# Stores of layer norms and of gated activations on other queues, and one sum of squares on the tensor engine

## The chip, the cores and the metric

The kernel runs on one core of a Trainium2 chip. A core has a tensor engine (PE, with its weight loads shown apart as PEld), a vector engine (DVE), a scalar engine (ACT), GpSimd (POOL) and a sync engine (SP) that only begins transfers. Each engine works through one queue of instructions in order. A transfer (DMA) is begun by an instruction on the queue of SP, ACT or POOL, and is then carried by 16 DMA engines that all queues share. The metric is the device time of one execution in microseconds (us). Three runs of the kernel before gave 3619.58, 3623.87 and 3626.42 us, median 3623.87 us.

## The reference, cut to what matters

Two layers are applied to two sequences, of 1040 and 272 positions (16 meta tokens ahead of each), with 1024 channels, all in float32. Layer 0 mixes tokens by a long convolution, layer 1 by attention. In each layer the mixer's result is added to the input and normed, and then a gated MLP with a convolution over three positions is added and normed again:

```python
h = layer_norm(DEEPNORM_ALPHA * h + m, ln1_g[i], ln1_b[i])
f = conv_ffn(h, ffn_w_in[i], ffn_conv_w[i], ffn_conv_b[i], ffn_w_out[i])
h = layer_norm(DEEPNORM_ALPHA * h + f, ln2_g[i], ln2_b[i])

def conv_ffn(x, w_in, conv_w, conv_b, w_out):
    h = x @ w_in
    g, a = jnp.split(h, 2, axis=-1)
    g = dwconv3(g, conv_w, conv_b)
    return (jax.nn.gelu(g, approximate=False) * a) @ w_out

def layer_norm(x, g, b):
    mu = mean(x); xc = x - mu; var = mean(xc * xc)   # over the 1024 channels
    return xc * rsqrt(var + LN_EPS) * g + b
```

## The kernel before, in words

Channels lie on the 128 partitions, in 8 tiles (index k or f), and positions in the free dimension. The positions are cut into four chunks: p = 0 has two of 384 columns, p = 1 two of 272 (layer 0) or 258 (layer 1); c = 0, 1 says which of the two. Every matrix product is taken in three passes over a high and a low part of each factor (lines 288 to 290), so weights and activations are first split: a copy on ACT (line 259) makes the high part, a subtraction on DVE (line 260) the low one.

A layer's second half has three stages.

`out_proj` (line 847 loads, 851 adds) makes the input of the first norm. `window_norms` norms the chunks of one p, stores the normed tiles to DRAM (`xd`, line 868) and makes the 7 operands T of the block product. It runs as work in the background: its pieces are traced between the matrix products of the next stage.

`ffn_in` multiplies T by weights (loaded at line 920), with convolution and gelu, and gates: `store` multiplies on DVE (line 985) and stores the gated tile to DRAM (`hd`, line 987), four stores for each of the 22 blocks of a layer. The first four blocks are done for p = 0 alone and then for p = 1 alone, while the norm of p = 1 still runs.

`ffn_out` reads back `hd` (line 1026, tile `hraw`, three buffers) and loads weights (line 1022), splits both, and accumulates for c = 0 and then for c = 1. The second norm of a c runs in the background of what follows; its results go to `x2d` in layer 0 (line 1403, after a split into the next input) and to the output `y` in layer 1 (line 1411).

`layer_norm` itself: the mean by a product with a constant matrix (line 781), subtraction on DVE (786), squares on ACT (788), their sum over the 8 tiles on POOL, one after another (790), the mean of that on PE (796), the reciprocal root in small steps on ACT and DVE (820 to 825), a broadcast on PE (804), and for each tile a scaling on DVE (809), a bias on ACT (810) and `done(f)`, which begins the store. `pin` puts a PE instruction behind everything that was traced on PE before it. The last two norms, of c = 1 in layer 1, have nothing beside them: the kernel ends with them.

The order on each queue is made by a planner, which issues the instructions by priority as they come ready in its own model; tiles, buffers and semaphores are its work as well. In the kernel before all of these stores are begun by SP, on the same queue as every load of weights and of `hraw`; the only transfers that POOL begins are in the first stage (lines 467 and 542), and ACT begins none.

Of the kernel before, what the change touches and what calls it, by code (L numbers as in the profile page):

```python
# [17 lines left out]
KC = D // 128  # L18
# [229 lines left out]
class Trunk:  # L248
# [519 lines left out]
        if f:  # L768
            self.nc.vector.tensor_tensor(out=sm, in0=A[0] if f == 1 else sm, in1=A[f], op=ALU.add)

    def layer_norm(self, A, sm, idx, done):


        nc = self.nc
        v = nc.vector
        n = sm.shape[-1]
        b = self.lnp[:, idx + 1]
        ps = lambda: self.pps.tile([128, 512], F32, tag="ln", name=self.n("ln"), bufs=2)[:, :n]
        mu = ps()
        pin = self.tc.keep_in_program_order  # L780
        pin(nc.tensor.matmul(out=mu, lhsT=self.o1024, rhs=sm, start=True, stop=True))
        nb = -(-n // 128)
        m = 2 * -(-n // (2 * nb))
        at = [min(m * i, n - m) for i in range(nb)]
        for f in range(KC):
            v.tensor_tensor(out=A[f], in0=A[f], in1=mu, op=ALU.subtract)
            sq = sm if f == 0 else self.tp(n)
            nc.scalar.activation(out=sq, in_=A[f], func=AF.Square)  # L788
            if f:
                nc.gpsimd.tensor_tensor(out=sm, in0=sm, in1=sq, op=ALU.add)  # L790
            if f == 3:
                yield 1.5
        yield 8
        var = ps()
        for i, o in enumerate(at):
            x = nc.tensor.matmul(out=var[:m, i:i + 1], lhsT=sm[:, o:o + m], rhs=self.o1024[:, 0:1], start=True, stop=True)
            if i == 0:
                pin(x)
        small = lambda: self.tmp.tile([128, 4], F32, tag="rs", name=self.n("rs"), bufs=6)[:m, :nb]
        r = self.rsqrt(small, var[:m, :nb], nb, self.eps[:m, 0:1], LN_EPS)  # L800
        yield 1.5
        rb = ps()
        for i, o in enumerate(at):
            x = nc.tensor.matmul(out=rb[:, o:o + m], lhsT=r[:, i:i + 1].to_broadcast([m, 128]), rhs=self.ident[:m, :m],
                                 start=True, stop=True)
            if i == 0:
                pin(x)
        for f in range(KC):
            v.scalar_tensor_tensor(out=A[f], in0=A[f], scalar=self.lng2[:, idx, f:f + 1], in1=rb, op0=ALU.mult, op1=ALU.mult)
            nc.scalar.activation(out=A[f], in_=A[f], func=AF.Identity, bias=b[:, f:f + 1])  # L810
            done(f)
            if f == 3:
                yield 3
# [42 lines left out]
    def window_norms(self, l, lay, p, A, sms, idx):  # L856

        nc = self.nc
        v = nc.vector
        n, n2 = lay.n[p], lay.n[p] + 2  # L860

        def done(c):
            o = lay.start[p][c]

            def f(k):
                for z in lay.zeros(p, lay.window(p, c)[0], n2):
                    nc.gpsimd.memset(A[c][k][:, z:z + 1], 0.0)
                nc.sync.dma_start(out=self.xd[l][:, k, o:o + n], in_=A[c][k][:, 1:n + 1])
            return f

        gens = [self.layer_norm(A[c], sms[c], idx, done(c)) for c in range(2)]
        while gens:
            for g in list(gens):
                x = next(g, None)
                if x is None:
                    gens.remove(g)
                else:
                    yield x / 2
        T = self.T[p] = {x: [] for x in PRODUCTS}
        left = 16  # L880

        def operand():
            nonlocal left
            left -= 1
            if left >= 0:
                return self.act.tile([128, 2, n2], F32R, tag=f"y{p}", name=self.n("T"), bufs=16)
            return self.tx.tile([128, 2, n2], F32R, tag=f"t{p}x", name=self.n("T"), bufs=(12, 16)[p])

        for q in range(2):
            for x in PRODUCTS:  # L890
                T[x].append((operand(), operand()))
            for j in range(2):
                k = 2 * q + j
                b11, b21, b12, b22 = A[0][k], A[0][k + 4], A[1][k], A[1][k + 4]
                put = lambda x, src: self.split(src, T[x][q][0][:, j], T[x][q][1][:, j])
                put("B11", b11)
                t2, t1 = self.tp(n2), self.tp(n2)
                v.tensor_tensor(out=b12, in0=b22, in1=b12, op=ALU.subtract)
                v.tensor_tensor(out=t2, in0=b12, in1=b11, op=ALU.add)
                put("B21", b21)  # L900
                put("T2", t2)
                v.tensor_tensor(out=t1, in0=b22, in1=t2, op=ALU.subtract)
                put("T1", t1)
                yield 2
                put("T3", b12)
                put("B22", b22)
                v.tensor_tensor(out=t2, in0=b21, in1=t2, op=ALU.subtract)
                put("T4", t2)
                yield 2
# [31 lines left out]
    def ffn_in(self, l):  # L941


        nc = self.nc
# [16 lines left out]
        for m, pairs in jobs:  # L961
            cw = self.cwf[:, l, m]
            st = {p: {} for p in pairs}
            for p in pairs:
                self.need(p)
            for x in PRODUCTS:
                while len(ready) < 4:
                    r = next(ops, None)
                    if r is None:
                        break  # L970
                    ready.append(r)
                wt = ready.pop(0)
                for p in pairs:
                    n, S = lay.n[p], st[p]
                    n2, T = n + 2, self.T[p][x]
                    mine = slice(1, n + 1)
                    key = dict(B11="a", T2="a", T3="a", T4="a", B21="b", T1="c", B22="c")[x]
                    new = x in ("B11", "B21", "T1")
                    if new:
                        S[key] = bank()[:, :n2]  # L980
                    ps = S[key]
                    self.mm3(ps, [(wt[k][0], wt[k][1], T[k // 2][0][:, k % 2], T[k // 2][1][:, k % 2]) for k in range(4)], new, again=not new)

                    def store(g, val, c):
                        v.tensor_tensor(out=g, in0=g, in1=val, op=ALU.mult)
                        o = 384 if p else 0
                        nc.sync.dma_start(out=self.hd[l][c, m, :, o:o + n], in_=g)

                    if x in ("B11", "T2", "T1"):
                        S[x] = self.tp(n2)  # L990
                        nc.scalar.copy(out=S[x], in_=ps)
                    elif x == "B21":
                        v.tensor_tensor(out=S["B11"], in0=S["B11"], in1=ps, op=ALU.add)
                        g = S["g"] = hidden(n)
                        self.conv3(g, S["B11"], n, cw)
                        nc.scalar.activation(out=g, in_=g, func=AF.Gelu)
                    elif x == "T3":
                        v.tensor_tensor(out=S["T1"][:, mine], in0=S["T1"][:, mine], in1=ps[:, mine], op=ALU.add)
                    elif x == "B22":
                        v.tensor_tensor(out=S["T2"], in0=S["T2"], in1=ps, op=ALU.add)  # L1000
                        g = hidden(n)
                        self.conv3(g, S["T2"], n, cw)
                        nc.scalar.activation(out=g, in_=g, func=AF.Gelu)
                        store(g, S["T1"][:, mine], 1)
                    else:
                        store(S["g"], ps[:, mine], 0)
                    self.tick(0.0055 * n2)

    def ffn_out(self, l, idx, done):
# [31 lines left out]
        for c in range(2):  # L1041
# [25 lines left out]
                        self.tick(0.9 * (k1 - k0))  # L1067
            for p in range(2):
                A = [z[:, 384 * p:384 * p + lay.n[p]] for z in C]
                self.later(("x", 2 * p + c), self.layer_norm(A, sms[p], idx, done(p, c, A)))  # L1070


    def qkv(self, common, later):
# [323 lines left out]
    def to_x(self, p, c, A):  # L1397
        lay = LAYERS[0]
        o, n, at = lay.start[p][c], lay.n[p], c * lay.n[p]

        def f(k):
            self.split(A[k], self.x[p][0][k][:, at:at + n], self.x[p][1][k][:, at:at + n])
            self.nc.sync.dma_start(out=self.x2d[:, k, o:o + n], in_=A[k])
        return f

    def to_y(self, p, c, A):
        s = p and c
        o = LAYERS[1].start[p][c] - LAYERS[1].col(s, T0)

        def f(k):  # L1410
            self.nc.sync.dma_start(out=self.a[f"y_{s}"][:, k, o:o + LAYERS[1].n[p]], in_=A[k])
        return f


# [18 lines left out]
```

## Time and profile before

| | us |
|---|---|
| median of three runs | 3623.87 |
| the profiled execution's own time | 3623.7 |
| its span (first to last instruction) | 3621.5 |
| PE busy | 3425.1 |
| DVE busy | 2290.0 |
| ACT busy | 1707.8 |
| POOL busy | 509.0 |

The times below are counted from the start of the span. Busy time is the time in which an engine executes; an instruction that begins a transfer takes time on its queue and is not counted as busy, except on POOL. "Idle before" an instruction is how long its engine had nothing to do, with what ended that. SPq, ACTq and POOLq are the queues of these engines.

### The profile page before, as it was taken

The numbers are of one execution on the slowest core, as the hardware profiler recorded it, in microseconds if no ns is written. First come the engines' busy times: TensorE is split into PE (matmuls) and PEld (weight loads), VectorE is DVE, ScalarE is ACT, GpSimd is POOL, SyncE is SP. The second block draws the span as 40 slices with busy tenths as digits, with TensorE's granted clock in tenths as the row PEclk, the third lists the DMA queues.
The fourth block names the chain that finished last, engine by engine and source line by source line (L and its number), as shares of the span: only waits on it lengthen the run. The fifth ranks groups of instructions, "written<-read, shape, count | busy, mean of one in ns | idle before, by whom it ended". The sixth has DMA issues, their size and how long they took to land.

```text
span 3621.5 us, 61578 instructions
## 1 busy us (share of the span) xinstructions
PE 3425.1 (95%) x23000; PEld 3315.7 (92%) x23000; DVE 2290.0 (63%) x4624; ACT 1707.8 (47%) x3614; POOL 509.0 (14%) x626
## 2 busy tenths in 40 slices
PE   8999999999989999999899999999979999999986
PEld 7999999998879999999898988888979999999986
DVE  6555554664797666654667557776598666654645
ACT  4333333663465444433545447776375444433434
POOL 2434341110110000000102341110110000000101
PEclk8999999999989999999999999999989999999998
DMA  6222223544222212255565440001233222246575
GB/s 169 89 96 91 92 89 114 146 136 139 94 87 92 74 61 75 67 178 178 158 195 166 135 130 16 16 12 44 92 102 97 77 68 66 74 135 203 139 196 139
DMA packets 239741, 391.69 MB, mean 108 GB/s; under 512 B 30580, under 2 KB 134235, under 8 KB 239059
## 3 DMA queue, kind: packets, MB, share of 16 engines
q1 hardware_dynamic: 232659, 364.70, 33.4%
q0 software_dynamic: 6784, 23.07, 1.7%
q8 instruction: 180, 2.95, 0.3%
q14 instruction: 118, 0.97, 0.1%
HBM read 302.22 MB, written 78.84 MB: 105 GB/s over the span
## 4 chain that ended last, share of the span: by engine, by line
PE 63%; DVE 5%; ACT 4%; DMA 2%; POOL 1%; issue 1%; SPq 0%; POOLq 0%; ACTq 0%; DVEq 0%
PE mm L288 17%; PE mm L290 17%; PE mm L289 17%; PE pt L1263 2%; PE sc L288 1%; PE pv L1279 1%; PE pv L1280 1%; DVE w L260 1%; PE pv L1281 1%; PE sc L290 1%; PE sc L289 1%; POOL tp L790 1%; DVE T L260 1%; DMA hraw<-hd 1%; ACT C L810 1%
## 5 line engine op out<-in xcount | busy, mean ns | idle before, releaser
L288 PE MATMUL mm<-T,w 128*128 128x386 f32 (+2 forms) x2464 | 778.0, 316 | 34.4 <-ACT w L259 26.7
L260 DVE TENSOR_TENSOR w<-raw,w 128x512 fp32r<-128x512 f32 (+2 forms) x744 | 511.9, 691 | 437.8 <-ACT w L259 424.3
L259 ACT CAST w<-raw 128x512 fp32r<-128x512 f32 (+2 forms) x744 | 439.1, 593 | 729.2 <-PE mm L289 571.8
L290 PE MATMUL mm<-T,w 128*128 128x386 f32 (+2 forms) x2464 | 774.7, 315 | 3.7 <-DVE w L260 3.4
L289 PE MATMUL mm<-T,w 128*128 128x386 f32 (+2 forms) x2464 | 774.6, 314 | 0.0
L288 PE MATMUL mm<-y,w 128*128 128x386 f32 (+6 forms) x1664 | 543.9, 327 | 14.3 <-ACT y L259 10.2
L290 PE MATMUL mm<-y,w 128*128 128x386 f32 (+6 forms) x1664 | 531.1, 320 | 12.9 <-DVE w L260 12.8
L289 PE MATMUL mm<-y,w 128*128 128x386 f32 (+6 forms) x1664 | 532.5, 320 | 2.6 <-DVE y L260 1.2
L288 PEld LDWEIGHTS mm<-T,w 128*128 128x128 f32 x2464 | 468.3, 190 | 41.9 <-ACT w L259 31.1
L290 PEld LDWEIGHTS mm<-T,w 128*128 128x128 f32 x2464 | 467.7, 190 | 7.8 <-DVE w L260 7.5
L289 PEld LDWEIGHTS mm<-T,w 128*128 128x128 f32 x2464 | 468.9, 190 | 0.3
L288 PE MATMUL mm<-hq,w 128*128 128x328 f32 (+2 forms) x1408 | 440.7, 317 | 23.6 <-ACT hq L259 23.4
L289 PE MATMUL mm<-hq,w 128*128 128x328 f32 (+2 forms) x1408 | 444.3, 316 | 7.0 <-DVE hq L260 7.0
L290 PE MATMUL mm<-hq,w 128*128 128x328 f32 (+2 forms) x1408 | 443.5, 315 | 0.0
L790 POOL TENSOR_TENSOR tp<-tp,tp 128x384 f32<-128x384 f32 (+5 forms) x112 | 116.7, 1050 | 1836.3 <-ACT tp L788 1830.2
L288 PEld LDWEIGHTS mm<-y,w 128*128 128x128 f32 x1664 | 321.3, 193 | 19.0 <-ACT y L259 12.9
L290 PEld LDWEIGHTS mm<-y,w 128*128 128x128 f32 x1664 | 321.5, 193 | 14.8 <-DVE w L260 14.3
L289 PEld LDWEIGHTS mm<-y,w 128*128 128x128 f32 x1664 | 321.3, 193 | 8.2 <-DVE y L260 3.9
L288 PEld LDWEIGHTS mm<-hq,w 128*128 128x128 f32 x1408 | 268.6, 192 | 25.0 <-ACT hq L259 24.9
L289 PEld LDWEIGHTS mm<-hq,w 128*128 128x128 f32 x1408 | 270.5, 192 | 8.8 <-DVE hq L260 8.5
L290 PEld LDWEIGHTS mm<-hq,w 128*128 128x128 f32 x1408 | 270.0, 192 | 0.0
L260 DVE TENSOR_TENSOR hq<-hraw,hq 128x656 fp32r<-128x656 f32 (+1 forms) x220 | 187.1, 851 | 62.4 <-ACT hq L259 58.2
(210 smaller groups left out, 5759.5 us busy)
## 6 DMA issues: line engine op xcount, KB each, us to landing
raw<-in_w_fin SPq DMA_DIRECT2D x208, 256.0 KB
hraw<-hd SPq DMA_DIRECT2D x110, 328.0 KB
hraw<-hd SPq DMA_DIRECT2D x110, 321.0 KB
raw<-in_w_fout SPq DMA_DIRECT2D x88, 256.0 KB
hd<-g SPq DMA_DIRECT2D x88, 192.0 KB
raw<-in_w_fout SPq DMA_DIRECT2D x88, 192.0 KB
raw<-in_w_hin SPq DMA_DIRECT2D x48, 256.0 KB
kk<-kd SPq DMA_DIRECT2D x64, 192.0 KB
```

The lines of the kernel that those rows point to most:

```text
L259: self.nc.scalar.copy(out=h, in_=src)
L260: (self.nc.gpsimd if pool else self.nc.vector).tensor_tensor(out=l, in0=src, in1=h, op=ALU.subtract)
L288: mm(out=ps, lhsT=wh, rhs=xh, start=start and i == 0, stop=False, **skip)
L289: mm(out=ps, lhsT=wh, rhs=xl, start=False, stop=False, **skip)
L290: mm(out=ps, lhsT=wl, rhs=xh, start=False, stop=stop and i == last, **skip)
L790: nc.gpsimd.tensor_tensor(out=sm, in0=sm, in1=sq, op=ALU.add)
L810: nc.scalar.activation(out=A[f], in_=A[f], func=AF.Identity, bias=b[:, f:f + 1])
L1263: nc.tensor.transpose(pt[:kn, q0:q0 + m], pr[:m, 128 * j:128 * j + kn], self.ident[:m, :m])
L1279: mm(out=pv, lhsT=vh, rhs=ph[:kn, :nn], start=(jj == 0), stop=False)
L1280: mm(out=pv, lhsT=vh, rhs=pl[:kn, :nn], start=False, stop=False)
L1281: mm(out=pv, lhsT=vl, rhs=ph[:kn, :nn], start=False, stop=last)
```

## The change

The stores of normed tiles (`xd`, `x2d`, `y`: 64, 32 and 32 instructions) are begun by ACT instead of SP, those of gated tiles (`hd`, 176 instructions) by POOL instead of SP. `layer_norm` gets a flag, true for the second norm of layer 1 at p = c = 1 alone: there the 8 tiles of squares aren't summed on POOL; PE multiplies each by the constant column as it comes and adds up in PSUM, in three blocks of 86 positions, 24 products instead of 3.

```diff
-    def layer_norm(self, A, sm, idx, done):
+    def layer_norm(self, A, sm, idx, done, on_pe=False):
...
+        var = ps() if on_pe else None
         for f in range(KC):
             v.tensor_tensor(out=A[f], in0=A[f], in1=mu, op=ALU.subtract)
             sq = sm if f == 0 else self.tp(n)
             nc.scalar.activation(out=sq, in_=A[f], func=AF.Square)
-            if f:
+            if on_pe:
+                for i, o in enumerate(at):
+                    nc.tensor.matmul(out=var[:m, i:i + 1], lhsT=sq[:, o:o + m], rhs=self.o1024[:, 0:1], start=f == i == 0,
+                                     stop=f == KC - 1, skip_group_check=i > 0)
+            elif f:
                 nc.gpsimd.tensor_tensor(out=sm, in0=sm, in1=sq, op=ALU.add)
             if f == 3:
                 yield 1.5
         yield 8
-        var = ps()
-        for i, o in enumerate(at):
+        for i, o in enumerate(at if not on_pe else ()):
+            if i == 0:
+                var = ps()
             x = nc.tensor.matmul(out=var[:m, i:i + 1], lhsT=sm[:, o:o + m], rhs=self.o1024[:, 0:1], start=True, stop=True)
...
-                nc.sync.dma_start(out=self.xd[l][:, k, o:o + n], in_=A[c][k][:, 1:n + 1])
+                nc.scalar.dma_start(out=self.xd[l][:, k, o:o + n], in_=A[c][k][:, 1:n + 1])
...
-                        nc.sync.dma_start(out=self.hd[l][c, m, :, o:o + n], in_=g)
+                        nc.gpsimd.dma_start(out=self.hd[l][c, m, :, o:o + n], in_=g)
...
-                self.later(("x", 2 * p + c), self.layer_norm(A, sms[p], idx, done(p, c, A)))
+                self.later(("x", 2 * p + c), self.layer_norm(A, sms[p], idx, done(p, c, A), l == c == p == 1))
...
-            self.nc.sync.dma_start(out=self.x2d[:, k, o:o + n], in_=A[k])
+            self.nc.scalar.dma_start(out=self.x2d[:, k, o:o + n], in_=A[k])
...
-            self.nc.sync.dma_start(out=self.a[f"y_{s}"][:, k, o:o + LAYERS[1].n[p]], in_=A[k])
+            self.nc.scalar.dma_start(out=self.a[f"y_{s}"][:, k, o:o + LAYERS[1].n[p]], in_=A[k])
```

## Rows read from the trace of the kernel before

**Rows 1.** The page, busy time, share of the span and instructions of each engine.

```profile
PE 3425.1 (95%) x23000; PEld 3315.7 (92%) x23000; DVE 2290.0 (63%) x4624; ACT 1707.8 (47%) x3614; POOL 509.0 (14%) x626
```

**Rows 2.** Windows of 90 us: busy us (instructions) by engine, PE clock, DMA share, GB/s.

```profile
1170.00:1260.00 90.00, 90.00 (x595) 90.00 (x595) 56.93 (x107) 37.41 (x71) 0.00 (x0) 1.00 0.21 68
...
2610.00:2700.00 90.00, 73.20 (x471) 70.86 (x470) 85.44 (x186) 63.51 (x137) 18.73 (x48) 0.91 0.34 113
```

**Rows 3.** Waits of PE over the whole span: us in total, times, longest us.

```profile
PE mm L288 <- ACT w L259: 30.7, 12, 6.3
```

**Rows 4.** Waits of the SP queue over the whole span, same columns.

```profile
SPq L987 <- DVE g L985: 513.0, 121, 12.0
...
SPq L1411 <- DMA y<-C: 8.3, 5, 4.3
```

**Rows 5.** Timeline of SP, 3395 to 3460 us: start, us, instruction, count.

```profile
3427.22 15.97 SPq L1411 DMA_DIRECT2D y<-C  x16
3443.28 3.10 SPq L1026 DMA_DIRECT2D hraw<-hd  x2
```

**Rows 6.** Timeline of ACT, same place; in brackets the idle time before and its releaser.

```profile
3454.77 0.73 ACT L259 CAST hq<-hraw 128x642 fp32r<-128x642 f32 x1 [17.16 <-DMA hraw<-hd]
```

**Rows 7.** Timeline of PE, same place.

```profile
3455.55 0.64 PE L288 MATMUL mm<-hq,w 128*128 128x322 f32 x1 [13.81 <-ACT hq L259]
```

**Rows 8.** Windows of four chosen stretches, columns as in rows 2.

```profile
963.00:976.00 13.00, 10.56 (x84) 10.34 (x83) 12.03 (x26) 11.43 (x23) 0.79 (x8) 0.99 0.61 222
...
1026.00:1046.00 20.00, 16.27 (x94) 15.20 (x92) 19.58 (x49) 19.31 (x46) 1.85 (x24) 1.00 0.55 169
...
3442.00:3454.00 12.00, 0.00 (x0) 0.00 (x0) 0.00 (x0) 0.00 (x0) 0.00 (x0) 0.71 0.97 130
3454.00:3462.00 8.00, 6.22 (x26) 5.88 (x27) 4.72 (x7) 4.76 (x8) 0.00 (x0) 0.58 0.82 256
```

**Rows 9.** Timeline of SP where `ffn_in` of layer 1 ends.

```profile
3231.36 0.33 SPq L1026 DMA_DIRECT2D hraw<-hd  x1
3232.08 1.32 SPq L987 DMA_DIRECT2D hd<-g  x3
3233.45 3.95 SPq L1026 DMA_DIRECT2D hraw<-hd  x3
```

**Rows 10.** Line 987: durations in ns (least, median, most), first and last start.

```profile
L987 SPq DMA_DIRECT2D hd<-g x176: 319/327/2017, 1023.7 to 3233.0; - x176
```

**Rows 11.** Groups of POOL: busy us, mean ns, idle before.

```profile
L467 POOL DMA_DIRECT2D kd<-ko x56 | 31.4, 561 | 81.2 <-DVE ko L466 80.8 <-DVE ks L430 0.4
```

**Rows 12.** Groups of ACT, 963 to 976 us, same columns.

```profile
L810 ACT ACTIVATE A<-A,lnp 128x386 f32<-128x386 f32 x16 | 8.9, 610 | 3.9 <-DVE A L809 3.9
```

**Rows 13.** Timeline of ACT, same stretch.

```profile
964.99 2.14 ACT L810 ACTIVATE A<-A,lnp 128x386 f32<-128x386 f32 x4
967.03 0.50 ACT L259 CAST T<-A 128x386 fp32r<-128x386 f32 x1
```

**Rows 14.** Timeline of POOL, 139 to 144.5 us.

```profile
141.83 0.88 POOL L539 TENSOR_TENSOR u<-vt,u 128x320 f32<-128x320 f32 x1
143.01 0.58 POOL L542 DMA_DIRECT2D vd<-u  x1 [0.30 <-POOL u L539]
```

**Rows 15.** Timeline of POOL, the last two norms.

```profile
3587.28 9.53 POOL L790 TENSOR_TENSOR tp<-tp,tp 128x258 f32<-128x258 f32 x11 [169.00 <-ACT tp L788]
3597.80 3.13 POOL L790 TENSOR_TENSOR tp<-tp,tp 128x384 f32<-128x384 f32 x3 [0.99 <-ACT tp L788]
```

**Rows 16.** Timeline of PE, the last two norms.

```profile
3595.91 1.04 PE L796 MATMUL ln<-squares,tp 128*86 128x1 f32 x6 [9.37 <-POOL tp L790]
3600.98 1.44 PE L796 MATMUL ln<-squares,tp 128*128 128x1 f32 x6 [4.04 <-POOL tp L790]
```

**Rows 17.** Timeline of ACT, the last two norms.

```profile
3604.40 7.57 ACT L810 ACTIVATE C<-C,lnp 128x258 f32<-128x258 f32 x16 [1.23 <-DVE C L809]
```

**Rows 18.** Timeline of SP, the last two norms.

```profile
3604.94 9.59 SPq L1411 DMA_DIRECT2D y<-C  x16
```

## The prediction

> **What bounds the kernel now.** I begin with the page's busy times: PE works 3425.1 us of a span of 3621.5, the next engine, DVE, 2290.0 [rows 1]. So the kernel is bound by PE, and any gain has to come out of the 196 us in which PE stands still, or runs at its lower clock after a stand. The windows of 90 us say where these are not. In the middle of `ffn_in` PE is busy 90.00 of 90 us [rows 2]; the reader should hold that against the most striking row of SP's waits, 513.0 us in which SP's queue stood at the store of a gated tile until DVE had multiplied it [rows 4]. Those waits delay loads that nothing waits for; they are worth nothing. The stands lie at the seams: where the norms of `window_norms` run, DVE is busy 85.44 of 90 us and PE only 73.20 [rows 2], and PE's longest wait by kind is for weights that ACT has yet to cast, 30.7 us [rows 3].
>
> The third view is the timeline around the second norm of layer 1 at c = 0. SP begins 16 stores of `y` over 15.97 us, and only at 3443.28 the next load of `hraw` [rows 5]. ACT has that tile at 3454.77, after 17.16 us of idling [rows 6], and PE stood 13.81 us [rows 7]. Part of those 16 us SP itself waited for earlier stores to land (8.3 us in all) [rows 4]. [...] The last view is the end: after the last product the sums of squares of two chunks pass one after another through POOL, and PE waits 9.37 and 4.04 us for them [rows 16].
>
> **Part 1, stores of `y` at c = 0 (16, SP to ACT).** Removed from SP: 15.97 us between a load of weights and the next `hraw` [rows 5]. SP then reaches that load as soon as a `hraw` buffer is free, some 8 to 10 us earlier. What it can give is the stand of 13.81 us [rows 7] and, of the 8 us from 3454 to 3462 at clock 0.58 [rows 8], 8 x (1 - 0.58) = 3.4 us: at most 17.2. At least nothing, if the loads come no sooner (second rival). The stores remain to be carried, and the DMA engines are full in the stretch (share 0.97 [rows 8]), so the loads share with them. I take 10 us of the stand and 2 of the clock, -12.
>
> **Part 2, stores of gated tiles (176, SP to POOL).** In steady `ffn_in` 0: PE has no gap there [rows 2]. POOL pays about 0.56 us for each, as for its own stores in the first stage [rows 11], against 0.33 on SP [rows 10]; 176 x 0.56 = 99 us on an engine that is busy 0.00 in those windows [rows 2]. While the norm of p = 1 runs, a store waiting for DVE also holds back what POOL does for that norm. The first such store in layer 0 comes at 1023.7 [rows 10], when POOL has only the zeroing of columns left; I cost it at 0, at most 5 per layer if its waits push the norm. A gain lies at the end of `ffn_in`: after the first `hraw` load SP stands at three stores until 3233.4 before the second [rows 9], which could follow at 3231.7, 1.75 us earlier. PE needs two units to begin, so 0 to 1.75 per layer; I take 1.2, twice: -2.4.
>
> **Part 3, stores of `xd` and `x2d` (64 and 32, SP to ACT).** SP loses nothing that PE waited for, so only the cost counts, and the trace of before has no transfer begun by ACT. On SP one issue takes 0.33 us [rows 10]. Four biases of ACT in a row take 2.14 us, 0.51 us each in step [rows 13], though each lasts 0.61 [rows 12]: they overlap by 0.1. Lower bound 0: if another ACT instruction stands between bias and store, as a cast of T does already [rows 13], the 0.33 us pass while ACT executes. Upper bound: store straight behind its bias, which must first be finished, so the step is 0.61 + 0.33 = 0.94 instead of 0.51, +0.43 a store, 6.9 for a group of 16. The four groups of `xd` fall where ACT has no room (busy 11.43 of 13 us and 19.31 of 20) with DVE as full (12.03 and 19.58) [rows 8], so what ACT loses there is on the path. For `x2d` a cast always follows the bias, so I keep it near the lower bound. I take 1 us for each of the four `xd` groups and 1 for each of the two of `x2d`, nearer to the lower end since T's casts and the weights' casts mix in: +6.
>
> **Part 4, the end.** POOL now sums 14 tiles: the last three take 3.13, 1.04 each [rows 15]. With the 258 columns on PE, seven of 1.04 remain, 7.3 us from about 3588.5, done near 3596 instead of 3600.9: at best -5. PE takes 1.04 us for three such products [rows 16], so 8 x 1.04 = 8.3 us in all, beside POOL. But the mean of the other chunk is pinned behind the first four tiles' products, 4 x 1.04, and may find its PSUM buffer taken; at worst the second chunk starts 5 us later than now and nothing is won, or 1 lost. I take -3. The 16 last stores of `y` go to ACT, which now needs 7.57 us for their biases [rows 17] while SP needs 9.59 [rows 18]. On ACT 0 if they hide, and 16 x 0.43 = 6.9 if each follows its bias, less the 2 us by which SP already trails. I take +3.
>
> **Sum.** -12 - 2.4 + 6 - 3 + 3 = -8.4 us. The span becomes 3621.5 - 8.4 = 3613.1; the profiled execution took 2.2 us more than its span, so 3615.3. The median of the runs shown, 3623.87, is 0.2 above the profiled execution; I predict 3615.5 us.
>
> **The rivals.**
>
> *First: ACT as the serial issuer (slower).* For it: where POOL stores what it has just made, the store stands directly behind its producer and waits 0.30 us for it [rows 14]. If the planner does the same on ACT, the upper bound of part 3 holds: 4 x 6.9 = 27.5 for `xd`, half a group, 3.5, for `x2d`, 5 at the end, and the gain of part 1 shrinks to 7, since ACT's casts of `hraw` stand behind the same stores. 27.5 + 3.5 + 5 - 7 - 2.4 - 3 = +23.6: 3647.5. It decides from 29 of the 64 `xd` stores on (12.4 us / 0.43), from where the sum is above zero. Against it: DVE steps through these tiles hardly faster than ACT, so the planner has casts of T and of weights ready to put between. [...]
>
> *Second: the loads come no sooner (no change).* With the DMA engines at 0.97 while moving only 130 GB/s [rows 8], the loads may have to wait for the same stores whoever begins them, and for the landing of earlier ones, as SP did [rows 4]. Then part 1 is 0 and the sum +3.6: 3627.5. Against it: `hraw` was begun late, at 3443.28, behind all 16 stores on one queue [rows 5]. [...]
>
> *Third: the sum on PE gains nothing.* PE's order (pin, buffer) puts the second chunk's mean late, and +1 stands in place of -3: 3619.5. For it: eight groups of products of 1.04 us are slower than the step of the squares, so PE becomes the chain. Against: POOL's adds are the slowest step now [rows 15].
>
> **How the numbers follow.** Forecast 0.40, first rival 0.27, second 0.20, third 0.13. About 0.2%, 7.2 us, is what a measurement of this kernel can tell from no change. The forecast lies just beyond that and holds 0.36 of faster, 0.04 of no change; the first rival 0.24 slower and 0.03 between; the second 0.15 no change, 0.03 slower, 0.02 faster; the third 0.10 no change, 0.03 faster. That is faster 0.41, same 0.32, slower 0.27. The forecast's own range is 3601 to 3622: all of parts 1 and 2, the best end and hidden stores on one side (-17.2 - 3.5 - 5 + 3 = -22.7), a quarter of the gains on the other. For 8 in 10 it must reach to the first rival: 3600 to 3647.
>
> **What would show it.** Right: SP has an `hraw` load soon after 3435 and PE's stand there is under 5 us; ACT's biases keep a step near 0.5 us where `xd` and `y` are stored; windows of steady `ffn_in` are unchanged; the last sum of POOL ends before 3597 by today's clock. Wrong: ACT steps near 0.94 with its stores between, and longer PE waits for casts of w or T after the window norms (first rival); a stand of over 10 us after the `y` stores (second); or PE's mean of the last chunk beginning after 3590 (third).

## The result, and the profile after

The changed kernel takes 3644.86 us (median of 4, 3637.94 to 3648.62) against 3622.25 for the kernel before: ratio 1.0059, interval [1.0041, 1.0078]. I had forecast 3615.5, faster; it is 22 us slower. The time lies near the first rival's 3647.5, outside the forecast's own range (3601 to 3622) and inside the wider one (3600 to 3647), but its terms are not that rival's.

The page after, busy time, share and instructions of each engine:

```profile
PE 3454.1 (95%) x23042; PEld 3338.7 (92%) x23042; DVE 2289.7 (63%) x4624; ACT 1708.3 (47%) x3614; POOL 599.3 (16%) x795
```

The page has PE 29.0 us busier than in [rows 1], while the span grew by 20.9. Of the 29.0, 7.2 lie behind the last product of `ffn_out`, where the sum of squares adds 42 small instructions. The other 21.8 are for the same products, and in that part PE stood no longer (162.8 us, before 165.2): it worked longer, and its clock says why. Up to that point PE was busy for 157.9 us at the lower clock, 0.50 of full, before for 117.7; 40.2 us more at half speed make 20.1 (worked out from the two traces). Where it happened is found by counting PE's instructions in both traces and asking how much later the same-numbered one starts (worked out from the two traces, us):

| stretch (time in before) | after | `xd` alone on ACT | `x2d` alone on ACT | `hd` alone on POOL | `y` alone on ACT |
|---|---|---|---|---|---|
| window norms, layer 0 (920 to 1150) | +6.7 | +6.5 | +0.3 | +0.4 | +1.0 |
| `ffn_in` (1150 to 1560) | +0.4 | +0.4 | 0.0 | 0.0 | 0.0 |
| seam to `ffn_out` (1560 to 1650) | +1.8 | +1.5 | +1.6 | +1.2 | -0.5 |
| second norm, c = 0 (1740 to 1920) | +3.0 | +1.2 | +2.6 | +1.3 | +0.1 |
| second norm, c = 1 (1920 to 2140) | +4.0 | -0.5 | +5.8 | +0.9 | +3.2 |
| window norms, layer 1 (2600 to 2800) | +6.6 | +6.5 | +0.1 | +1.1 | +1.3 |
| `y` stores of c = 0 (3400 to 3520) | -3.4 | -0.4 | -0.2 | -0.2 | -3.7 |
| the end (from 3520) | +1.6 | +1.8 | +0.7 | +1.1 | +1.7 |

The columns to the right are the first four experiments, and their off-diagonal entries show how far equal code wanders: 1 to 3 us. The stretches left out wander too (the first 920 us, which no edit touches, came out 1.8 to 3.6 us earlier in these five), so a column does not add up to its version's ratio below. What stands out is the diagonal, the end apart: +1.6 and +1.7 there are no more than in the three columns whose end is unchanged (+0.7 to +1.8). The windows after, columns as in [rows 2] (steady `ffn_in`, the norms of layer 1, the stand at the `y` stores and what follows it):

```profile
1170.00:1260.00 90.00, 90.00 (x593) 90.00 (x592) 54.77 (x101) 38.32 (x74) 6.42 (x12) 1.00 0.20 64
...
2615.78:2822.46 206.68, 180.33 (x1160) 172.32 (x1159) 184.12 (x374) 126.54 (x267) 36.18 (x72) 0.93 0.31 100
3459.00:3471.00 12.00, 1.08 (x4) 0.98 (x5) 1.10 (x2) 5.21 (x11) 0.00 (x0) 0.65 0.80 158
3471.00:3479.00 8.00, 8.00 (x50) 8.00 (x50) 2.62 (x5) 1.67 (x4) 0.00 (x0) 0.89 0.94 162
```

The norms of layer 1 in the kernel before, cut at the same 1160 instructions of PE:

```profile
2600.05:2800.11 200.06, 174.20 (x1160) 167.62 (x1159) 183.35 (x374) 125.97 (x267) 28.22 (x56) 0.95 0.32 103
```

Steady `ffn_in` is untouched, with POOL now 6.42 us busy beginning stores. At the norms of layer 1 the other engines do the same work as before, and PE is idle as long (26.3 us, before 25.9); it is busy 6.1 us longer for the same products at a lower mean clock (0.93, before 0.95). The stand at the `y` stores has a granted clock of 0.65, and what follows it 0.89 where [rows 8] had 0.58. Next, ACT in the first norm of layer 0 (start, us, instruction, count, idle before), which answers [rows 13]:

```profile
961.98 0.62 ACT L816 ACTIVATE A<-A,lnp 128x386 f32<-128x386 f32 x1 [3.35 <-DVE A L815]
...
969.64 1.13 ACT L816 ACTIVATE A<-A,lnp 128x386 f32<-128x386 f32 x2 [0.40 <-DVE A L815]
970.29 0.83 ACTq L874 DMA_DIRECT2D xd<-A  x2
971.17 1.13 ACT L816 ACTIVATE A<-A,lnp 128x386 f32<-128x386 f32 x2 [0.41 <-ACT A L816]
...
976.32 0.50 ACT L259 CAST T<-A 128x386 fp32r<-128x386 f32 x1
```

Two biases, then two stores, then 0.40 us idle: a step of 1.53 for two tiles, 0.77 for one, where [rows 13] had 0.51. That is +0.26 a store, between my bounds of 0 and 0.43. But the last row matters more: T's first cast comes 14.3 us after the first bias. The same place at the `y` stores of c = 0, answering [rows 5 to 7] (SP, ACT and PE in order of time):

```profile
3439.72 0.33 SPq L1032 DMA_DIRECT2D hraw<-hd  x1
...
3456.79 0.33 SPq L1032 DMA_DIRECT2D hraw<-hd  x1
...
3460.29 3.91 ACTq L1417 DMA_DIRECT2D y<-C  x2
3464.24 1.02 ACT L816 ACTIVATE C<-C,lnp 128x384 f32<-128x384 f32 x2 [4.22 <-DMA y<-C]
...
3469.16 0.71 ACT L259 CAST hq<-hraw 128x642 fp32r<-128x642 f32 x1
...
3469.92 0.64 PE L288 MATMUL mm<-hq,w 128*128 128x322 f32 x1 [11.06 <-ACT hq L259]
```

SP begins `hraw` at 3456.79, which is 3434.0 on the clock of before and so 9.3 us earlier than 3443.28. PE stands 11.06 us nevertheless: ACT can't cast, because its queue stands at the stores, some of which wait for an earlier store of `y` to land (ACT idles 4.22 us there). The early load has no part in that stand: the tile cast at 3469.16 is the one loaded from 3439.72 on, which had landed at 3442.9 (worked out by taking loads and casts in order), and the load of 3456.79 is cast two tiles later. The end, answering [rows 15 to 17]:

```profile
3606.30 3.68 PE L792 MATMUL ln<-squares,tp 128*86 128x1 f32 x24 [1.03 <-ACT tp L789]
3609.84 1.63 PE L781 MATMUL ln<-tp,squares 128*128 128x384 f32 x2
...
3613.22 7.44 POOL L795 TENSOR_TENSOR tp<-tp,tp 128x384 f32<-128x384 f32 x7 [172.13 <-ACT tp L789]
...
3624.12 0.91 ACT L816 ACTIVATE C<-C,lnp 128x258 f32<-128x258 f32 x2 [1.23 <-DVE C L815]
...
3634.44 1.12 ACT L816 ACTIVATE C<-C,lnp 128x384 f32<-128x384 f32 x2 [0.42 <-ACT C L816]
```

### The profile page after: what moved, and what is told of

It is laid out like the page before. It is cut to its first block, busy times and chain, and to the rows that moved or that the text cites. A ratio compares the mean times of both kernels' runs of the same rounds, so it can differ in the third digit from the quotient of the medians.

```text
span 3642.4 us, 61743 instructions
## 1 busy us (share of the span) xinstructions
PE 3454.1 (95%) x23042; PEld 3338.7 (92%) x23042; DVE 2289.7 (63%) x4624; ACT 1708.3 (47%) x3614; POOL 599.3 (16%) x795
## 3 DMA queue, kind: packets, MB, share of 16 engines
q8 instruction: 181, 2.97, 0.3%
## 4 chain that ended last, share of the span: by engine, by line
PE 62%; DVE 6%; DMA 3%; ACT 3%; POOL 1%; issue 1%; ACTq 0%; SPq 0%; POOLq 0%; DVEq 0%
PE mm L288 17%; PE mm L290 17%; PE mm L289 17%; PE pt L1269 2%; PE sc L288 1%; DMA hraw<-hd 1%; DVE w L260 1%; PE pv L1285 1%; PE pv L1286 1%; PE sc L290 1%; PE sc L289 1%; PE pv L1287 1%; POOL tp L795 1%; DVE T L260 1%; DMA raw<-in_w_fin 1%
## 5 line engine op out<-in xcount | busy, mean ns | idle before, releaser
L288 PE MATMUL mm<-T,w 128*128 128x386 f32 (+2 forms) x2464 | 779.8, 317 | 29.6 <-ACT w L259 17.1
L288 PEld LDWEIGHTS mm<-y,w 128*128 128x128 f32 x1664 | 324.8, 195 | 23.5 <-ACT y L259 14.1
L290 PEld LDWEIGHTS mm<-y,w 128*128 128x128 f32 x1664 | 325.6, 196 | 16.6 <-DVE w L260 16.1
L289 PEld LDWEIGHTS mm<-y,w 128*128 128x128 f32 x1664 | 325.3, 196 | 7.9 <-DVE y L260 4.1
L993 POOL DMA_DIRECT2D hd<-g x176 | 94.4, 540 | 1006.0 <-DVE g L991 991.3
```

The lines of the kernel that those rows point to most:

```text
L288: mm(out=ps, lhsT=wh, rhs=xh, start=start and i == 0, stop=False, **skip)
L289: mm(out=ps, lhsT=wh, rhs=xl, start=False, stop=False, **skip)
L290: mm(out=ps, lhsT=wl, rhs=xh, start=False, stop=stop and i == last, **skip)
L993: nc.gpsimd.dma_start(out=self.hd[l][c, m, :, o:o + n], in_=g)
```

## The experiments

All ratios are to the kernel before, run on the same chip in turn.

**Each part alone.** One engine's name changed in the kernel before:

```diff
-                nc.sync.dma_start(out=self.xd[l][:, k, o:o + n], in_=A[c][k][:, 1:n + 1])
+                nc.scalar.dma_start(out=self.xd[l][:, k, o:o + n], in_=A[c][k][:, 1:n + 1])
```

> The kernel before with one edit: the 64 stores of xd begun by ACT. Theory A (ACT pays for each start, some 0.26 us in step, and its casts of T and of weights come later by that): of the 21 us lost, the two traces place +6.7 at the window norms of layer 0 and +6.5 at those of layer 1, so this kernel alone is 13 us slower than before (11 to 15), ratio about 1.0036. Theory B (the loss at the window norms comes from the first gated stores on POOL, which fall in the same 100 us): 0 to +3 here. Theory C (the losses are chance of PE's clock and don't belong to single parts): within 4 us of before, on either side.

Measured 1.0033 [1.0022, 1.0044], some 12 us; its trace has +6.5 us at each of the two window norms.

> The kernel before with one edit: the 32 stores of x2d begun by ACT. Theory A: the two traces place +3 at the second norm of layer 0 for c = 0 and +4 at that for c = 1, both beside x2d stores, so +7 us (5 to 8). Theory B (gated stores on POOL) and theory C (chance): within 2 us of before.

 (the same edit to the line that stores `x2d`)

Measured 1.0028 [1.0018, 1.0038], some 10 us (6.5 to 13.8 by the interval), which holds theory A's 7. Its trace has +2.6 and +5.8 us at the two norms; versions with `x2d` left on SP reach +3.5 at the second.

> The kernel before with one edit: the 176 stores of gated tiles begun by POOL. Theory A: the steady part of ffn_in showed no loss in the changed trace, and only the two seams to ffn_out remain (+1.8 and +0.5), so 0 to +2 us. Theory B: +10 us or more, since the first blocks' stores wait on POOL's queue between the pieces of the norm. Theory C: within 4 us.

 (SP to POOL in the line that stores `hd`)

Measured 0.9999 [0.9990, 1.0008]: nothing.

> The kernel before with one edit: the 32 stores of y begun by ACT. Theory A (the stand behind the y stores of c = 0 shrank only by what SP's queue saved, since ACT's casts of hraw now stand behind the stores and these wait for earlier ones to land): -3.4 us at that place and 0 to +5 at the end, so -3 to +2. Theory C: within 4 us. My recorded sum had -12 + 3 = -9 for these edits.

 (SP to ACT in the line that stores `y`)

Measured 0.9995 [0.9987, 1.0004]; the stand shrank from 13.81 to 10.35 us.

**The sum on PE alone** (all stores back on SP).

> The changed kernel with all stores back on SP: what is left of the change is the sum of squares on PE for the last chunk. My recorded term was -3. The end of the changed trace is 1.5 us longer than before, while the y stores on ACT alone left it as it was: so the sum on PE costs some 1.5 us (0 to +3), because the 24 products come one by one behind the squares and the root of the last chunk begins no earlier (theory F). Theory G (the longer end belongs to the stores on ACT in company with the sum): -3 to 0 here.

Measured 1.0009 [1.0000, 1.0017]. From the last product of `ffn_out` to the first bias of the end it took 20.34 us, before 20.79: 0.4 gained instead of 3 or 5. The five ratios add to +0.64%, the whole change measured +0.59%, so the parts add, and theories B and C are out: `xd` and `x2d` on ACT are the loss.

**ACT, or SP's relief?** The same stores on POOL:

> The kernel before with one edit: the 64 stores of xd begun by POOL instead of SP. It relieves SP's queue exactly as the version on ACT did (which was 12 us slower) and loads nothing onto ACT. Theory A (what costs is the place on ACT's queue, ahead of its casts): within 3 us of before. Theory D (what costs is that SP, freed of the stores, begins weight loads earlier and these collide with the stores in the DMA engines): some 12 us slower again.

Measured 1.0004 [0.9995, 1.0013].

> The kernel before with one edit: the 32 stores of x2d begun by POOL instead of SP. On ACT they cost 10 us. Theory A (the cost is the place on ACT's queue): within 3 us of before, as it was for xd on POOL. Theory D (SP freed of them): 10 us slower again.

Measured 0.9993 [0.9984, 1.0002]. And the whole change with these two on POOL:

> The changed kernel with xd and x2d begun by POOL instead of ACT; gated stores on POOL, y on ACT and the sum on PE as changed. Theory A (the changed kernel's 21 us are the 12 and 10 of xd and x2d on ACT): within 5 us of before, ratio 1.000. If the parts hinder each other (POOL now begins 272 transfers and sums the norms): 5 us slower or more.

Measured 0.9994 [0.9984, 1.0005]. SP's relief costs nothing; beginning `xd` and `x2d` on ACT is all of the 22 us. ACT in the version with `xd` on POOL has the order of before:

```profile
965.29 0.62 ACT L810 ACTIVATE A<-A,lnp 128x386 f32<-128x386 f32 x1 [3.35 <-DVE A L809]
...
966.64 2.14 ACT L810 ACTIVATE A<-A,lnp 128x386 f32<-128x386 f32 x4
968.68 0.50 ACT L259 CAST T<-A 128x386 fp32r<-128x386 f32 x1
```

T's first cast is 3.4 us after the first bias. In the changed kernel the planner lets every bias and store pass first, and it comes at 14.3; PE's first product with T follows 35.2 us after the first bias instead of 29.4 (worked out from the traces). PE pays for the delay in clock and not in standing: with `xd` alone on ACT it is idle 25.6 and 26.3 us at the two window norms, before 25.1 and 25.9, but busy at 0.50 for 27.4 and 27.6 us, before 16.9 and 16.5 (worked out from the traces).

**Is it the store's wait for its bias?** The store traced two tiles late:

```diff
-                nc.sync.dma_start(out=self.xd[l][:, k, ...], in_=A[c][k][...])
+                late[c].append(k)
+                while len(late[c]) > (2 if k < KC - 1 else 0):
+                    j = late[c].pop(0)
+                    nc.scalar.dma_start(out=self.xd[l][:, j, ...], in_=A[c][j][...])
```

> The kernel before with the 64 stores of xd begun by ACT, each traced two tiles after its own bias. Theory A1 (the cost is the wait of a store for the bias just ahead of it: ACT's step was 0.77 us a tile with the stores between, 0.51 without): with the wait gone the 0.33 us of a start pass while ACT executes, so the loss falls from 12 to under 4 us. Theory A2 (the cost is that every start takes ACT's queue and the planner puts the casts of T and of weights behind them, whenever the bias was done): 8 us slower or more.

Measured 1.0054 [1.0042, 1.0067]. The window norms have +6.5 and +6.6 us in its trace, as with the wait; the rest of the growth of its span lies in stretches without these stores. A1 falls. ACT at the end of the group:

```profile
974.55 0.60 ACT L810 ACTIVATE A<-A,lnp 128x386 f32<-128x386 f32 x1
...
975.06 0.60 ACT L810 ACTIVATE A<-A,lnp 128x386 f32<-128x386 f32 x1
...
975.56 0.60 ACT L810 ACTIVATE A<-A,lnp 128x386 f32<-128x386 f32 x1
975.62 4.46 ACTq L872 DMA_DIRECT2D xd<-A  x3
980.12 0.51 ACT L259 CAST T<-A 128x386 fp32r<-128x386 f32 x1 [3.96 <-DMA xd<-A]
```

The steps are back at 0.51, yet T's first cast is 15.8 us after the first bias (964.33): the stores still stand ahead of the casts, and the queue waits there for an earlier store to land (ACT idles 3.96 us).

**Is it their order?** As many stores on ACT, traced between the casts of T:

```diff
-                nc.sync.dma_start(out=self.xd[l][:, k, ...], ...)
+                if c == 1 and k == 0:
+                    keep(c, k)          # nc.scalar.dma_start of tile k of chunk c
...
                 put("B11", b11)
+                keep(0, k)
+                if k < 3:
+                    keep(1, k + 1)
...
                 put("B22", b22)
+                keep(0, k + 4)
+                keep(1, k + 4)
```

> The kernel before with the 64 stores of xd begun by ACT, but traced between the casts of T that follow the norm instead of behind each bias (the tile that is overwritten is stored a step ahead). ACT begins as many transfers as in the version that lost 12 us. Theory A2 (the loss is the order: biases and stores ahead of T's casts, whose first came 13.5 us after the first bias instead of 3.4): within 4 us of before. Theory A3 (64 times 0.33 us of ACT's queue in a stretch without room is the loss, in any order): 8 us slower or more.

Measured 1.0012 [1.0003, 1.0021], some 4 us: two thirds of the loss gone with all 64 starts still on ACT. T's first cast is 3.4 us after the first bias again:

```profile
963.38 0.62 ACT L810 ACTIVATE A<-A,lnp 128x386 f32<-128x386 f32 x1 [3.35 <-DVE A L809]
...
966.77 0.50 ACT L259 CAST T<-A 128x386 fp32r<-128x386 f32 x1
966.82 0.35 ACTq L872 DMA_DIRECT2D xd<-A  x1
```

So the order (A2) is most of it, and ACT's DMA queue as such, which these stores still use, can be no more than the rest. The 4 us left may be the starts themselves; they are at the edge of how far equal code wanders (+4.4 at the norms of layer 0, where versions without `xd` on ACT reach +2.7, and +0.5 at those of layer 1).

**What `x2d` on ACT does** is seen in its trace. ACT:

```profile
1986.38 0.41 ACT L259 CAST y<-C 128x272 fp32r<-128x272 f32 x1
1988.63 0.27 ACT L259 CAST vh<-ln 128x128 fp32r<-128x128 f32 x1 [1.84 <-PE ln L1128]
1988.79 0.62 ACT L810 ACTIVATE C<-C,lnp 128x384 f32<-128x384 f32 x1
1990.96 0.27 ACT L259 CAST vh<-ln 128x128 fp32r<-128x128 f32 x1 [1.56 <-PE ln L1128]
```

In the kernel before, at the same place:

```profile
1988.66 0.92 ACT L259 CAST y<-C 128x384 fp32r<-128x384 f32 x2
1989.48 0.62 ACT L810 ACTIVATE C<-C,lnp 128x384 f32<-128x384 f32 x1
1989.99 0.25 ACT L259 CAST vh<-ln 128x128 fp32r<-128x128 f32 x1
```

Biases now stand behind casts of `vh` that wait for PE (1.84 and 1.56 us), so ACT idles in a stretch where before it ran without a gap (from 1985 to 1990 it is busy 2.57 us, before 5.00). PE's work there breaks into pieces (busy 2.97 us of the 5 from 1995), and its granted clock is 0.50 from 2000 on, before 1.00. Windows of the same version, and of the kernel before:

```profile
1995.00:2000.00 5.00, 2.97 (x14) 2.08 (x13) 3.36 (x10) 4.77 (x17) 0.00 (x0) 0.84 0.55 194
2000.00:2005.00 5.00, 5.00 (x24) 4.74 (x23) 1.38 (x7) 2.60 (x7) 0.77 (x1) 0.50 0.38 94
2005.00:2010.00 5.00, 5.00 (x23) 4.96 (x23) 2.87 (x9) 1.44 (x3) 2.27 (x3) 0.50 0.31 86
2010.00:2015.00 5.00, 5.00 (x21) 5.00 (x20) 2.74 (x6) 1.28 (x3) 4.38 (x5) 0.50 0.47 142
```

```profile
1995.00:2000.00 5.00, 4.70 (x17) 4.11 (x17) 4.78 (x10) 3.38 (x10) 1.94 (x3) 0.52 0.63 174
2000.00:2005.00 5.00, 5.00 (x44) 4.92 (x43) 3.31 (x13) 1.72 (x4) 1.44 (x2) 1.00 0.48 151
```

PE is busy all 15 us from 2000, at a granted clock of 0.50, with 68 products where the kernel before has 123 (44, 38, 41). That is 55 of 123 of 15 us, about 6.7, and shows how PE's busy time rises while nothing stands. In the whole stretch from 1920 to 2140 of the table PE is busy at 0.50 for 20.4 us here and 20.2 in the changed kernel, before for 5.3, and in no version with `x2d` on SP or POOL for more than 13.0 (worked out from the traces). That the order on ACT sets this off is read from the trace; no run put that order back, as was done for `xd`.

**The `y` stores of c = 0.** On POOL, out of the way of SP and ACT alike:

> The kernel before with one edit: the 32 stores of y begun by POOL instead of SP. Theory A (on ACT the gain at the second norm of layer 1 for c = 0 was cut to 3.7 us because ACT's casts of hraw stood behind stores that waited for landings): POOL has nothing behind it there, so SP begins hraw some 10 us earlier, ACT casts it at once, and the stand of 13.81 us falls to 4 or less: 9 to 13 us faster, ratio 0.9970. Theory E (the DMA engines are the bound there, share 0.97, whoever begins the stores): no more than the 4 us of the version on ACT, ratio 0.9990.

Measured 0.9997 [0.9988, 1.0005]. SP, ACT and PE:

```profile
3434.60 0.33 SPq L1026 DMA_DIRECT2D hraw<-hd  x1
...
3448.12 0.73 ACT L259 CAST hq<-hraw 128x642 fp32r<-128x642 f32 x1 [10.04 <-DMA hraw<-hd]
...
3448.90 0.64 PE L288 MATMUL mm<-hq,w 128*128 128x322 f32 x1 [6.69 <-ACT hq L259]
```

The load begins 8.7 us earlier than in [rows 5] with no queue in its way, and takes 13.5 us until its cast. The stand is halved, a gain of 4.8 us at that place. At the end, where POOL too begins the stores, part of it is lost again: +3.9 us, where versions with the end unchanged have +0.7 to +2.6. A start takes POOL 0.54 us in this trace and SP 0.33 [rows 10]; that this makes the difference is my estimate. Then the stores held back:

```diff
             nc.sync.dma_start(out=r, in_=self.hd[l][c, kp, :, :N2])
+            self.late += bool(self.held)
+            if self.late > 6 and self.late % 2 == 0 and self.held:
+                self.held.pop(0)()      # one store of y, c = 0
```

> The kernel before; the 16 stores of y for c = 0 stay on SP, but each is held back and begun behind a load of hraw, one at every second load, some 12 us after the norm and later. Theory E (the stand of 13.81 us is the DMA engines' time for 16 stores ahead of the loads, whoever begins them: 10.35 us were left with the stores on ACT, 6.69 on POOL): the stand goes to under 3 us and the low clock behind it with it, 11 to 16 us faster, ratio 0.9963, since the DMA engines have room later (share 0.65 to 0.76 from 3460 us on). Theory E2 (the loads are slow of themselves there, because hd and the weights are read at 0.97 of the engines with or without stores): 0 to 4 us.

Measured 0.9985 [0.9976, 0.9994], but the edit did not take: the planner put the stores ahead of the loads, which waited for a buffer, and PE stood 14.33 us. What moved the time by 0.15% I can't see in the trace; I take it as a measure of what such a ratio is worth. With `keep_in_program_order` around the store, so that it stays behind the load on SP:

> The kernel before; each of the 16 stores of y for c = 0 is tied on SP's queue behind a load of hraw, the first some six loads after the norm's first result, then one at every second load. Theory E (the stand of 13.81 us is the DMA engines' time for 16 stores that stand ahead of the loads): it goes to under 3 us, 11 to 16 us faster in the trace at that place, ratio 0.9963. Theory E2 (the loads of hraw are slow of themselves there): stand over 8 us, 0 to 5 us faster.

Measured 0.9944 [0.9930, 0.9958]. SP and ACT, then windows as in [rows 8]:

```profile
3441.98 1.77 SPq L1027 DMA_DIRECT2D hraw<-hd  x2
...
3444.91 0.73 ACT L260 CAST hq<-hraw 128x642 fp32r<-128x642 f32 x1 [0.92 <-DMA hraw<-hd]
```

```profile
3442.00:3454.00 12.00, 12.00 (x81) 11.99 (x81) 8.27 (x13) 7.29 (x13) 0.00 (x0) 1.00 0.96 271
3454.00:3462.00 8.00, 8.00 (x55) 8.00 (x54) 3.60 (x5) 2.78 (x5) 0.00 (x0) 1.00 1.00 251
```

There is no stand and no low clock; PE gains 16.8 us at that place. The DMA engines are as full as in [rows 8] (0.96 against 0.97) but move 271 GB/s instead of 130: a full share said only that they were occupied.

**The sum on PE, after the other chunk's mean:**

```diff
-        var = ps() if on_pe else None
+        var = None
+        if on_pe:
+            var = self.pps.tile([128, 512], F32, tag="mm", name=self.n("mm"))[:, :n]
+            yield 0          # the other chunk's mean is traced here
```

> The kernel before with the sum of squares on PE for the last chunk as in the change, but with the mean of the other chunk traced ahead of the 24 products, and these in another PSUM tag. Theory F (the change gains nothing because that mean came 7.3 us later, at 3593.01 instead of 3585.73, behind the first 12 products): POOL starts its seven sums some 7 us earlier and the first bias of the end comes 4 to 5 us earlier, so 4 us faster than before and 7 faster than the sum on PE as it was. Theory F2 (PE's products or the squares are the chain whatever the order): no more than 1 us.

Measured 0.9977 [0.9966, 0.9988]. PE, POOL and ACT:

```profile
3585.25 1.32 PE L781 MATMUL ln<-tp,squares 128*128 128x258 f32 x4 [1.60 <-DVE tp L769]
...
3588.34 7.46 POOL L798 TENSOR_TENSOR tp<-tp,tp 128x384 f32<-128x384 f32 x7 [170.29 <-ACT tp L792]
...
3600.83 7.47 ACT L819 ACTIVATE C<-C,lnp 128x384 f32<-128x384 f32 x16 [2.20 <-DVE C L818]
```

All four products of the two means come first, POOL ends at 3595.8, and the first bias comes 17.2 us after the last product of `ffn_out` (worked out), not 20.8: 3.6 of the 8 us measured are accounted for, and the next runs bear out no more than these.

**Together:**

> The version just named together with the sum of squares on PE behind the mean of the other chunk (8 us faster by itself). If the two gains add, as places 130 us apart should: theory E 3607 us or less, 17 to 24 us faster than before, ratio 0.9940; theory E2 some 10 us, 0.9972.

Measured 0.9939 [0.9924, 0.9953], 3607.95 us, in the range of theory E. But the sum on PE adds only 2.6 us to the 3610.57 of the version just named, measured beside it, and not 8.

> As the version just named, and the 16 stores of x2d for c = 0 are tied behind loads of hraw in the same way in layer 0, where PE stood 6.31 us in the trace of before. Theory E: another 4 to 8 us. If that stand is not theirs (theory E2, or DVE's splits): 0 to 2.

Measured 0.9935 [0.9920, 0.9949], 3607.18 us: E2 for `x2d`, whose 6.31 us stand ends with a split on DVE and stayed. Both beat both kernels.

## Why the prediction was wrong

**Part 3 (forecast +6, measured +22) is the step that failed.** I priced a start by what it adds to ACT's step, 0 to 0.43, and put `xd` near the lower end "since T's casts and the weights' casts mix in". The step's price was inside the bounds (0.26, 4.1 a group). But the casts didn't mix in: the planner moved them behind all biases and stores. I had priced an instruction and not the new order of what stands behind it, though the queue was named in the part; and the delay came out as 11 us more of PE at half clock at each of the two window norms, a term that the part doesn't have. For `x2d` "a cast always follows the bias" was true, and beside the point: by its trace what cost was a bias behind a cast that waits for PE, and then 15 us of PE at half clock. The first rival had the sign and the place (`xd`), but its price, 0.43 for each store, was not the mechanism: with the step at 0.51 the loss was no smaller. Its "29 of the 64" leaves out its own 3.5 and 5 us; with them its sum is above zero from 10 stores on (3.9 / 0.43).

**Part 1 (forecast -12, measured -3.4)** failed in "10 us of the stand". That SP reaches the load 8 to 10 us earlier was right (9.3), but on ACT it did not bear on the stand, which ended with the cast of a tile that had landed 26 us before. Both objections I had weighed are true at once: on ACT the casts of `hraw` stand behind the stores (first rival), and off ACT the load itself is slow beside 16 stores (second rival, 13.5 us). My bound of 17.2 for this stand (some 0.7 of it counted twice, as PE stood until 3455.55 in the windows from 3454) was right: 16.8 came once the stores were behind the loads instead of beside them. Changing who begins the stores gave less: in the POOL version the load began 8.7 us earlier, took 13.5 us until its cast instead of 11.5, and so was cast 6.7 us earlier.

**Part 2 (forecast -2.4, measured 0 within 0.1%)**: steady `ffn_in` cost nothing, as priced, and each start took POOL 0.54 us. At the seam the second load did come sooner, and PE's stand shrank in layer 1 from 4.84 to 4.21 us only, since it waits for the first load to land (ACT idles 2.73 us for that landing, before 3.36).

**Part 4 (forecast 0; measured +1.6, within what equal code wanders)** came out by other terms. The -3 failed by the third rival's cause: PE took the mean of the other chunk at 3609.84, which is 3590.5 on the clock of before, behind the first 12 products, so POOL's seven sums began late and ended at 3620.66. I had named that cause and given it 0.13. The stores on ACT slowed the last 16 biases from 7.57 us [rows 17] to 11.44 (3624.12 to 3635.56), +3.9. How much of that reached the end is not shown: from the first of these biases to the end of the span it is 18.3 us, before 17.1, and 17.7 to 19.3 in versions whose end is unchanged.

**The signs** read as written: `hraw` early (right), stand under 5 us (wrong, 11.06), biases at 0.5 (wrong, 0.77), steady windows unchanged (right), POOL's last sum before 3597 (wrong, 3601.3 on the clock of before). Of the signs of being wrong, the first rival's did not show (ACT's step at 0.77 and not 0.94, and PE's waits for casts of w fell from 30.7 to 24.0 us); the second's did, a stand of over 10 us, but on ACT with the first rival's cause; the third's did (3590.5).

## What to carry to other kernels

Before a transfer is moved to a busy in-order queue, list what stands behind it there and ask whether the planner will reorder that queue; the price of the start itself may be the smallest part. Here 272 starts on POOL's queue, where nothing waited for the stores, cost nothing (ratio 0.9994); with the last stores of the kernel on POOL, at 0.54 us a start, the end was 3.9 us longer, against 0.7 to 2.6 where it was unchanged. And if a load is late beside stores that nobody waits for, put the stores behind the loads; changing who begins them gave about a quarter of what changing their order gave (3.7 us on ACT and 4.8 on POOL, against 16.8).

## What the runs showed of the hardware that I had not expected

In the changed kernel a store on ACT's queue held the bias behind it until its own wait was over. The second of two stores begins at 970.79, when its bias has just ended (970.76), and the next bias only at 971.17, when the start of 0.33 us is over.

The long stands, 3.91 us for two stores of `y` and 4.46 for three of `xd`, are something else. The stores of `y` by line in the changed kernel (ns: least, median, most):

```profile
L1417 ACTq DMA_DIRECT2D y<-C x32: 338/339/2451, 3450.5 to 3635.6; - x32
L1417 ACTq EVENT_SEMAPHORE  x21: 17/17/17, 3452.5 to 3635.5; - x21
```

A start takes 0.34 us; between the two starts of `y` at 3460.29 and 3463.86 stands an instruction of the program (`EVENT_SEMAPHORE`, 3463.80) that waits, on the semaphore that the second store will signal, until an earlier transfer on it has landed: the last signal of the store begun at 3453.56 came at 3463.78 (worked out from the trace). So this stand comes of how the program shares its semaphores among transfers, and that of `xd` also ended with the landing of an earlier store; a limit of the chip behind them is not shown.

With `x2d` alone on ACT, PE was busy 15 us on end at a granted clock of 0.50 after a stretch in which it worked 2.97 of 5 us; a busy PE in the page was no proof that it ran at speed. And the DMA engines showed nearly the same share, 0.97 in the kernel before and 0.96 with the `y` stores behind the loads, at 130 and at 271 GB/s.
